# An encoder layer on one core: 35 softmax normalisations on GpSimd, one more pair of projections by half products, and another order of the work

## The chip, the core and the metric

The kernel runs on one core of a Trainium2 chip. Its engines are TensorE (PE, matrix products), VectorE (DVE), ScalarE (ACT) and GpSimd (POOL); SyncE (SP) only issues DMAs, as GpSimd also does. The engines run on their own and wait for each other by semaphores. The time is device microseconds of one execution, and for a kernel the median over its runs.

## What is computed

One layer with two attention mixers side by side, a gated merge, and a SwiGLU block, on 512 tokens of 1024 channels in float32. Cut to what matters here:

```python
proj = h @ w_in[l]                                   # queries, keys, values of both mixers
o_a = windowed_gqa_sink(qa, ka, va, a_sink[l])       # 16 heads, |i-j| <= 128, a learned sink per head
o_b = dilated_mixture(qb, kb, vb)                    # 4 head slots, three dilations each
gates = jax.nn.sigmoid(h @ w_gate[l] + b_gate[l])    # 2 x 1024 channels
mixed = g_a * (o_a @ w_br_a[l]) + g_b * (o_b @ w_br_b[l])
h = layer_norm(DN_ALPHA * h + mixed @ w_out[l], ...)
f = (silu(h @ w_ff_gate[l]) * (h @ w_ff_up[l])) @ w_ff_down[l]
h = layer_norm(DN_ALPHA * h + f, ...)
```

## The kernel before

**Precision.** Every float32 factor is split into a high part that PE takes and a low part (`split`, `parts`: a copy on ScalarE or VectorE, and a subtraction on VectorE, L558, L413, L387). A product of two factors is then three matrix products: high by high, high by low, low by high (L537 to L539, L659 to L661 and so on).

**Units.** The weights come as units of 128 output columns. A unit is computed either alone (`feat_k`, L537 to L539: 8 blocks of the inner dimension x 3 products of 512 columns), or two units at a time by seven half products in place of eight (`pair_x`, L659 to L661: 7 x 12 products of 256 columns). A pair needs sums of weights, which are made by VectorE or by DMAs of GpSimd that add on arrival (L401, L624), and sums of results on VectorE.

**Mixer A.** `unit_a` handles four heads and 128 queries, 16 times. For each head: scores on PE (L903, L904); GpSimd writes the sink's value into a column of the tile (L1065); VectorE adds the mask and takes the row's extreme (L1067); ScalarE takes the exponential and its sum (L1071). When all four heads are there, VectorE takes the reciprocals (L1074), and `normalise` multiplies each head's block by its factor, on ScalarE (L1006) or on VectorE (L1008). Then PE transposes the four blocks together, one piece of 128 keys after the other (`turned_probs`, L1018), ScalarE and VectorE split what comes out (L387, L1023), and PE multiplies by the values (L1084, L1085). GpSimd's queue sends the result to memory (L1091).

**Mixer B.** `unit_b` does one head slot, four times, with eight blocks to normalise; its transposes are L1018 and L1033.

**After the mixers.** `gate` computes a gate unit and its tanh; the second half of the gates is parked in memory until it is used. `branch_a` and `branch_b` multiply the mixers' outputs by their weights and by the gates; then come the output projection (L1549 to L1551), the layer norm, and the SwiGLU block with its own half products (L1759 to L1761, L1970 to L1972).

**What sets the order.** The program is first recorded as operations with the tiles that they read and write. `Program.run` then walks through them with a table of costs and gives each operation a place on an engine: of those whose inputs are ready and whose buffers fit, the one with the lowest priority number. Where an operation lists several engines, the first one free takes it. So the order on each engine is fixed when the program is built, and every engine works through its own in that order. The string `ORDER` names the steps: `P:` and `D:` are pairs by half products (with `D:` their sums are made by DMA), `q`, `k`, `Q`, `K` projections, `g` gates, `R` and `r` rotary turns, `A0` to `A3` four blocks of mixer A, `B0` to `B3` the slots of mixer B, `O` fetches of A's output. The number behind `@` shifts a step's priorities; `BRANCHES` names the order of the branch tiles.

Of the kernel before, what the change touches and what calls it, by code (L numbers as in the profile page):

```python
# [15 lines left out]
P = 128  # L16
# [35 lines left out]
BIAS = 0.2  # L52
SPARE, SPARE2 = (4, 12)
ROOMS = {2: dict(whl=16), 3: dict(whl=20, ws=8)}
# [32 lines left out]
ORDER = """  # L87
X@-11 VA@-23 q2@-799 q1@-877 P:q3,g@-124 R@-106 D:k1,q4@-31 R@155 P:q5,Q01@-843 A0@-168 D:q6,q7@-47 D:g,g@-34 r@631 P:g,Q00@-22 L@-4 A2@-96
D:g,K00@-31 A1@-48 R@187 V12@-20 P:g,K01@-67 R@-5 P:Q02,K02@-28 A3@-55 V0@55 R@5 B0@-7 B1@11 O@25 O@35 P:K10,Q10@-39 O@-13 O@-54 K11@-34 R@24
O@11 P:Q12,Q11@-30 g@28 K12@-12 O@950 g@25 r O@43 P:g,g@-2 B2@-525 O@-304 B3@21 g@-29 P:g,g@-32 g@-8  # L90
"""
FORMS = -255.0
VAL = 140.0
OA_AFTER = (1, 0, 0, 0, 0, 1, 0, 0)
# [9 lines left out]

BRANCHES = "a0 a1 a2 a3 a4 b0 a5 b1 b2 a6 b3 b4 a7 b5 b6 b7"

# [31 lines left out]
class Program:  # L138


    def __init__(self, limits):
        self.limits = limits
        self.used = {k: 0 for k in limits}
        self.ops = []
        self.writer, self.readers = {}, {}
        self.T = 0.0
        self.spare = SPARE
        self.strict = self.hold = False
        self.rooms = {}

# [4 lines left out]
    def op(self, alts, fn, reads=(), writes=(), prio=0.0, after=(), abs_prio=None, moves=0.0, extra=0, table=None):  # L155
# [29 lines left out]
        self.ops.append(o)  # L185
        return o

    def fits(self, o):
# [18 lines left out]
    def run(self):  # L207
# [27 lines left out]
        while n_left:  # L235
# [13 lines left out]
            while progress:  # L249
                progress = False  # L250
                for e in engines:
# [19 lines left out]
                    for b in o.bufs:  # L271
                        if b.tile is None:
                            if b.keys[0] in self.rooms:
                                b.room = self.rooms[b.keys[0]].popleft()
# [70 lines left out]
def hybrid_layer(ctx: ExitStack, tc: tile.TileContext, wpack, xT, xtok, sink, bgate,  # L345
# [24 lines left out]
    def bank(cls):  # L370
        return Buf("bank", cls, lambda r: psum.tile([P, S], F32, tag=f"bank{r}", bufs=1, name=name("ps")))
# [120 lines left out]
    for j in range(2):  # L492
        for w, u in (("k", U_KA), ("q", U_QA), ("v", U_VA), *((i, U_GATE + 8 + i) for i in range(N_ALONG))):
            first[w, j] = half_unit_by(u, j, ((0, S),) if j else ALONG_CUTS if w in range(N_ALONG) else CUTS, FIRST[w, j])
# [52 lines left out]
    def feat_x(ps, wu):  # L547
        for k in range(KD):
            feat_k(ps, wu, k, XM, xtok_of)
# [208 lines left out]

    def in_sbuf(u):

        ps, t = bank("dense"), slot()
        feat_x(ps, unit(u))
        op([(ACT, act(S, True))], lambda e: copy(ACT, halves(t.t), back(ps.t)), reads=[ps], writes=[(t, 1), (t, 2)], prio=EV)
        return t
# [238 lines left out]
    def normalise(p_of, tok, n, f_of, ftok):  # L1003
        def go(e):
            if e == ACT:
                nc.scalar.activation(p_of(), p_of(), AF.Copy, scale=f_of())  # L1006
            else:
                nc.vector.tensor_scalar(p_of(), p_of(), f_of(), None, op0=ALU.mult)  # L1008

        op([(ACT, act(n, extra=1)), (DVE, dve(n, True, 0.06))], go, reads=[tok, ftok], writes=[tok])  # L1010

# [271 lines left out]
    def gate_of(f, t):  # L1283
        gz[f] = t
        op([(ACT, act(S, False, 1))], lambda e: nc.scalar.activation(
            t.t, t.t, AF.Tanh, bias=bg.t[:, f:f + 1], scale=0.5), reads=[(t, 1), (t, 2), bg], writes=[t], prio=EV)
        if f in AWAY:
            put_away(f)
# [6 lines left out]
    def gate(f, ps=None):  # L1295
        if ps is None:
            ps = bank("dense")
            feat_x(ps, unit(U_GATE + f))
        t = slot()
        gz[f] = t  # L1300
        op([(ACT, act(S, True, 1))], lambda e: nc.scalar.activation(
            halves(t.t), back(ps.t), AF.Tanh, bias=bg.t[:, f:f + 1], scale=0.5),
           reads=[ps, bg], writes=[t], prio=EV)
        if f in AWAY:
            put_away(f)
# [6 lines left out]
    def dense_k(u, nt):  # L1312
        ps = bank("dense")
        feat_x(ps, unit(u))
        return k_post(ps, nt) if nt else k_pairs(ps)

    psk, psq, psv = bank("dense"), bank("dense"), bank("dense")
    along = [bank("s") for _ in range(N_ALONG)]
# [11 lines left out]
    for f in range(N_ALONG):  # L1330
        gate(8 + f, ps=along[f])
    ka, qa = {0: k_near(psk, 4)}, {0: q_near(psq, 4, (0, 0))}
    load(mB, maskb, prio=0)
    env = {"gate": N_ALONG, "turn": [], "qs": {}, "ks": {}}

# [29 lines left out]
    def fetch_oa(k):  # L1365
# [8 lines left out]
        return split_of(st, [st], OA_SPLIT, h=Part(xa[k // 4], k % 4) if k >= N_XA else None, by_blocks=True)  # L1374

    def units_of(w):
        i = int(w[1:] or 0)
# [9 lines left out]
        if w[0] == "k":  # L1387
            return U_KA + i, lambda t: ka.update({i: k_post(t, 4)})
        f = (env["gate"] + 8) % 16
        env["gate"] += 1  # L1390
        return U_GATE + f, lambda t: gate_of(f, t)

    def step(w):
        if w == "X":
            x_forms()
        elif w == "L":
            op([(POOL, 0.0)], lambda e: pr.limits.update(ws=N_WS, whl=N_WHL), after=[env["mark"]])
# [31 lines left out]
        elif w[0] in "gG":  # L1429
            for _ in range(int(w[1:] or 1)):  # L1430
                gate((env["gate"] + 8) % 16)
                env["gate"] += 1
        elif w[0] in "QK":
# [16 lines left out]

    for w in ORDER.split():
        w, _, later = w.partition("@")
        pr.T += float(later or 0)
        step(w)
        pr.T -= float(later or 0)
# [5 lines left out]
    op([(POOL, 0.0)], free_all, after=lasts)  # L1461


# [12 lines left out]

    sa.extend(fetch_oa(k) for k in range(len(sa), 8))
    MA = moving(sa)
    sm, sb_ = {}, []

# [13 lines left out]
    def branch_b(f):  # L1494
        if not sb_:
            sb_.extend(split_of(t, [(t, 0), (t, 1)], OB_SPLIT) for t in obT)
        if f % 4 == 0:
            env["wu"] = unit(U_BRB + f // 4)
        MB = moving(sb_)
        ps = bank("dense")  # L1500
        for k in range(2):
            feat_k(ps, env["wu"], k, MB, lambda k: [sb_[k][0].tok, sb_[k][1]], nk=2, col=lambda k: (k, (f % 4) * P))
        mark = gated(8 + f, ps)
# [4 lines left out]

    names = BRANCHES.split()
    marks = []  # L1510
    for n, w in enumerate(names):
        k = 8 + int(w[1])
        if w[0] == "b":
            if k in away:
                fetch_gate(k, [*exps, marks[names.index("b%d" % (k - 11))]] if k > 10 else exps)
        marks.append((branch_a if w[0] == "a" else branch_b)(int(w[1])))
    for w, mark in zip(names, marks):
        env[w] = [mark]


# [594 lines left out]
```

## Time and profile before

| | |
|---|---|
| runs of the kernel before | median 724.24 us of 3 (723.83 to 725.03) |
| the profiled execution | 724.82 us |
| its span, first to last instruction | 723.0 us |
| granted TensorE clock | 0.998 |
| instructions | 14810 |
| HBM read, written | 119.69 MB, 8.39 MB |

The span is what the views divide up. A busy PE in them means that a matrix product is somewhere in its pipeline; the durations of successive products overlap, so the work is read from the distance of their starts. A row of the timeline is: start, duration, engine, line, operation, what it writes and reads, shape. Lines are those of the kernel before.

### The profile page before, as it was taken

What the parts mean: (1) busy time and instruction counts of PE and PEld (TensorE: products, weight loads), DVE (VectorE), ACT (ScalarE), POOL (GpSimd) and SP (SyncE); (2) the same over time, 40 slices, a digit from 0 to 9 for tenths busy, and PEclk for the clock granted to TensorE, in tenths of its full rate; (3) what the DMA queues carried; (4) which work ended last, traced back from release to release, by engine and by line L of the source; (5) the groups of instructions that cost most, each with busy time, mean ns of one, the idle gap of its engine ahead of it and who ended that gap; (6) DMA issues with size and microseconds to landing.
All of it is one profiled execution on the core that took longest, in us unless ns stands there. A gap on an engine that the chain in (4) does not pass through costs nothing.

```text
span 723.0 us, 14810 instructions
## 1 busy us (share of the span) xinstructions
PE 712.5 (99%) x4947; PEld 667.2 (92%) x4947; DVE 664.4 (92%) x1425; ACT 494.6 (68%) x1136; POOL 173.2 (24%) x347
## 2 busy tenths in 40 slices
PE   8999999999999999999999999999999999999996
PEld 6889999998999998988888999999999999999985
DVE  6998999999999989999958998999999999999987
ACT  5768889889878997767625666756567566666821
POOL 0113343322423591550020022121121201212000
PEclk9999999999999999999999999999999999999999
DMA  8978967887568789766690499776897868979402
GB/s 257 294 215 210 235 168 213 227 216 179 137 169 204 187 255 253 219 196 219 199 210 33 110 300 232 177 203 165 238 238 197 223 164 219 253 196 194 106 29 88
DMA packets 81275, 141.44 MB, mean 196 GB/s; under 512 B 11024, under 2 KB 15760, under 8 KB 81200
## 3 DMA queue, kind: packets, MB, share of 16 engines
q1 hardware_dynamic: 63472, 107.07, 46.3%
q0 software_dynamic: 17456, 33.30, 26.6%
q8 instruction: 39, 0.64, 0.4%
q14 instruction: 36, 0.29, 0.1%
q10 hardware_dynamic: 272, 0.13, 0.1%
HBM read 119.69 MB, written 8.39 MB: 177 GB/s over the span
## 4 chain that ended last, share of the span: by engine, by line
PE 90%; DMA 4%; DVE 3%; SPq 2%; ACT 1%; issue 0%; POOL 0%; DVEq 0%; ACTq 0%; POOLq 0%
PE ps L1761 10%; PE ps L1759 10%; PE ps L1760 9%; PE ps L659 5%; PE ps L661 5%; PE ps L660 5%; PE ps L537 4%; PE ps L538 4%; PE ps L539 4%; PE ps L1970 4%; PE ps L1972 4%; PE ps L1971 4%; PE ps L1018 3%; DMA sl<-wpack 3%; PE ps L1549 3%; PE ps L1551 3%
## 5 line engine op out<-in xcount | busy, mean ns | idle before, releaser
L387 ACT ACTIVATE sl<-sl 128x512 fp32r<-128x512 f32 (+3 forms) x457 | 253.8, 588 | 60.7 <-DVE sl L558 43.3
L558 DVE TENSOR_TENSOR sl<-sl,sl 128x512 fp32r<-128x512 f32 (+3 forms) x415 | 245.3, 628 | 6.0 <-ACT sl L387 5.0
L387 ACT ACTIVATE sl<-ps 128x256 f32<-128x256 f32 (+6 forms) x214 | 88.5, 440 | 76.6 <-PE ps L1761 53.0
L401 POOL DMA_DIRECT2D sl<-wpack x70 | 63.0, 931 | 319.1 <-DMA sl<-wpack 92.0
L1760 PE MATMUL ps<-sl,sl 128*128 128x256 f32 x352 | 96.8, 275 | 0.0
L1761 PE MATMUL ps<-sl,sl 128*128 128x256 f32 x352 | 96.8, 275 | 0.0
L1759 PE MATMUL ps<-sl,sl 128*128 128x256 f32 x352 | 96.8, 275 | 0.0
L1759 PE MATMUL ps<-x,sl 128*128 128x256 f32 x264 | 72.6, 275 | 0.0
L1760 PE MATMUL ps<-x,sl 128*128 128x256 f32 x264 | 72.6, 275 | 0.0
L1761 PE MATMUL ps<-x,sl 128*128 128x256 f32 x264 | 72.6, 275 | 0.0
L1759 PEld LDWEIGHTS ps<-sl,sl 128*128 128x128 f32 x352 | 67.6, 192 | 0.1
L1760 PEld LDWEIGHTS ps<-sl,sl 128*128 128x128 f32 x352 | 67.6, 192 | 0.1
L1761 PEld LDWEIGHTS ps<-sl,sl 128*128 128x128 f32 x352 | 67.6, 192 | 0.0
L537 PE MATMUL ps<-x,sl 128*128 128x512 f32 (+1 forms) x161 | 62.1, 386 | 0.7 <-ACT x L387 0.7
L539 PE MATMUL ps<-x,sl 128*128 128x512 f32 (+1 forms) x161 | 60.9, 378 | 0.0
L659 PE MATMUL ps<-sl,sl 128*128 128x256 f32 x208 | 57.8, 278 | 0.9 <-ACT sl L667 0.9
L661 PE MATMUL ps<-sl,sl 128*128 128x256 f32 x208 | 57.3, 276 | 0.0
L660 PE MATMUL ps<-sl,sl 128*128 128x256 f32 x208 | 57.2, 275 | 0.0
L558 DVE TENSOR_TENSOR sl<-sl,ps 128x512 f32<-128x512 f32 (+1 forms) x72 | 47.3, 661 | 9.0 <-PE ps L1972 5.8
L1759 PEld LDWEIGHTS ps<-x,sl 128*128 128x128 f32 x264 | 50.6, 192 | 0.4
L1760 PEld LDWEIGHTS ps<-x,sl 128*128 128x128 f32 x264 | 50.6, 192 | 0.4
L1761 PEld LDWEIGHTS ps<-x,sl 128*128 128x128 f32 x264 | 50.7, 192 | 0.0
(174 smaller groups left out, 2006.6 us busy)
## 6 DMA issues: line engine op xcount, KB each, us to landing
sl<-wpack SPq DMA_DIRECT2D x254, 256.0 KB
sl<-wpack POOLq DMA_DIRECT2D x70, 256.0 KB, 5.5
wf<-wpack SPq DMA_DIRECT2D x51, 256.0 KB
sl<-sl SPq DMA_DIRECT2D x56, 128.0 KB
wf<-wpack POOLq DMA_DIRECT2D x24, 256.0 KB, 5.3
oa<-sl POOLq DMA_DIRECT2D x32, 128.0 KB, 3.6
sl<-sl SPq DMA_DIRECT2D x72, 32.0 KB
gz<-sl SPq DMA_DIRECT2D x8, 256.0 KB
```

What stands on the lines that cost most here:

```text
L387: nc.scalar.activation(dst, src, AF.Copy)
L401: op([(POOL, 1.0)], lambda e: nc.gpsimd.dma_start(b.t, src2, accum_op=ALU.add), reads=[b], writes=[b], prio=prio, moves=1.65)
L537: mm(o, a, x0, start=(k == 0 and begins), stop=False, skip_group_check=split)
L538: mm(o, a, x1, start=False, stop=False, skip_group_check=split)
L539: mm(o, b, x0, start=False, stop=(k == nk - 1), skip_group_check=split)
L558: op([(DVE, dve(w))], lambda e: nc.vector.tensor_tensor(dst(), x(), y(), op=o), reads=reads, writes=writes, prio=prio)
L659: mm(o, wh, pairs(bh[k]()), start=(first and k == 0), stop=False, skip_group_check=True)
L660: mm(o, wh, pairs(bl[k]()), start=False, stop=False, skip_group_check=True)
L661: mm(o, wl, pairs(bh[k]()), start=False, stop=(k == 3), skip_group_check=True)
L1759: mm(o, wh, pairs(bh[k]()), start=(first and k == 0), stop=False, skip_group_check=True)
L1760: mm(o, wh, pairs(bl[k]()), start=False, stop=False, skip_group_check=True)
L1761: mm(o, wl, pairs(bh[k]()), start=False, stop=(k == 3), skip_group_check=True)
```

## The change

`normalise` gets GpSimd as a third engine, with a cost of 0.3 + 0.0012 per column in the planner. `ORDER` is another string: it has 14 pairs by half products in place of 13, it takes the branch tiles (`a0` to `b7`) into itself, and three gates (`g`, and a pair `P:g,g`) stand between branch tiles. The first key and query units (`k0`, `q0`) get steps of their own. `room_for` chooses among free PSUM banks, and all fetched parts of A's output go to plain slots. With the new costs and shifts, the planner puts out another order up to the output projection; the SwiGLU block's order is nearly the same as before. The core of the diff:

```diff
-SPARE, SPARE2 = (4, 12)
+SPARE, SPARE2 = (6, 12)
...
 ORDER = """
-X@-11 VA@-23 q2@-799 q1@-877 P:q3,g@-124 R@-106 D:k1,q4@-31 R@155 P:q5,Q01@-843 A0@-168 D:q6,q7@-47 D:g,g@-34 r@631 P:g,Q00@-22 L@-4 A2@-96
+X@37 P:q3,g@-229 R@-137 VA@-117 D:k1,q4@-42 k0@29 q0@243 R@461 P:q5,Q01@-516 q1@-615 A0@-190 D:q6,q7@-66 r@1309 D:g,g@-75 q2@-543 P:g,Q00@-19
...
+a5@-28 a2@-10 a3@-31 b2 b3@12 b1@-77 a6@-26 a7@-13 b4@23 b7@-75 b5@-71 b6@-207
 """
-FORMS = -255.0
+FORMS = -150.0
...
-STORE, OA, OA_SPLIT, OB_SPLIT, N_OA, N_XA = 0.0, -60.0, -140.0, -140.0, 4, 4
+STORE, OA, OA_SPLIT, OB_SPLIT, N_OA, N_XA = 0.0, -60.0, -140.0, -140.0, 4, 8
...
-BRANCHES = "a0 a1 a2 a3 a4 b0 a5 b1 b2 a6 b3 b4 a7 b5 b6 b7"
...
+    def room_for(self, b):
+        free = self.rooms[b.keys[0]]
+        if b.keys[0] != "bank":
+            return free.popleft()
+        room = next((r for r in free if self.whole.get(r)), free[0]) if b.keys[1] == "d" else free[0]
+        free.remove(room)
+        self.whole[room] = b.keys[1] in ("dense", "o", "d", "dff")
+        return room
...
             if e == ACT:
                 nc.scalar.activation(p_of(), p_of(), AF.Copy, scale=f_of())
+            elif e == POOL:
+                nc.gpsimd.tensor_scalar(p_of(), p_of(), f_of(), None, op0=ALU.mult)
             else:
                 nc.vector.tensor_scalar(p_of(), p_of(), f_of(), None, op0=ALU.mult)
 
-        op([(ACT, act(n, extra=1)), (DVE, dve(n, True, 0.06))], go, reads=[tok, ftok], writes=[tok])
+        op([(ACT, act(n, extra=1)), (DVE, dve(n, True, 0.06)), (POOL, 0.3 + 0.0012 * n)], go, reads=[tok, ftok], writes=[tok])
```

GpSimd's order around the second block of mixer A (`sl_913` is head 0 of the first block, `sl_971` to `sl_977` are the heads of the second), before:

```order
L624 DMA sl_715<-sl_741 128x512
L1065 COPY sl_971<-nsink 128x1
L1065 COPY sl_973<-nsink 128x1
L1065 COPY sl_975<-nsink 128x1
L1065 COPY sl_977<-nsink 128x1
L624 DMA sl_686<-sl_602 128x512
L624 DMA sl_792<-sl_715 128x512
```

The same place after the change; the lines are those of the changed kernel, where L1079 is the copy, L634 the DMA and L1020 the new branch of `normalise`:

```order
L634 DMA sl_716<-sl_742 128x512
L1079 COPY sl_971<-nsink 128x1
L1079 COPY sl_973<-nsink 128x1
L1079 COPY sl_975<-nsink 128x1
L1079 COPY sl_977<-nsink 128x1
L1020 ISA
L1020 TENSOR_SCALAR sl_913<-sl_913,st_926 128x256
L634 DMA sl_682<-sl_602 128x512
L634 DMA sl_792<-sl_716 128x512
L1105 DMA oa_1149<-sl_1129 64x4x128 x2
```

Two rows are new: the first normalisation on GpSimd, and ahead of it an ISA row, which in the built program is a reload of GpSimd's library (index 0). It stands once in the program. The two DMAs behind them are the sums of weights that stood there before.

PE's order at the first transposes of mixer A, before (`ps_1015` is a half product's bank):

```order
L659 MATMUL ps_1015<-sl_419,sl_861 128x256
L660 MATMUL ps_1015<-sl_420,sl_861 128x256
L661 MATMUL ps_1015<-sl_419,sl_862 128x256
L1018 MATMUL ps_1109<-ident,sl_913 128x128
L1018 MATMUL ps_1109<-ident,sl_918 128x128
L1018 MATMUL ps_1109<-ident,sl_922 128x128
L1018 MATMUL ps_1109<-ident,sl_924 128x128
L903 MATMUL ps_1119<-sl_712,sl_596 128x384
L904 MATMUL ps_1119<-sl_713,sl_596 128x384
```

And after, where L669 to L671 are the half products and L1032 the transposes:

```order
L670 MATMUL ps_1037<-x_252,sl_789 128x256
L671 MATMUL ps_1037<-x_244,sl_790 128x256
L1032 MATMUL ps_1062<-ident,sl_913 128x128
L1032 MATMUL ps_1062<-ident,sl_918 128x128
L1032 MATMUL ps_1062<-ident,sl_922 128x128
L1032 MATMUL ps_1062<-ident,sl_924 128x128
L1032 MATMUL ps_1068<-ident,sl_913 128x128
L1032 MATMUL ps_1068<-ident,sl_918 128x128
L1032 MATMUL ps_1068<-ident,sl_922 128x128
L1032 MATMUL ps_1068<-ident,sl_924 128x128
L669 MATMUL ps_979<-sl_330,sl_1001 128x256
```

The transposes of the first block now stand together and earlier: two groups of 12 half products and one head's two score products, which stood ahead of them, stand behind them.

More of the change, by code (lines that the diff above doesn't have):

```diff
@@ L148, in __init__ @@
         self.strict = self.hold = False
-        self.rooms = {}
+        self.rooms, self.whole = {}, {}
     @staticmethod
@@ L492, in hybrid_layer @@
     for j in range(2):
-        for w, u in (("k", U_KA), ("q", U_QA), ("v", U_VA), *((i, U_GATE + 8 + i) for i in range(N_ALONG))):
+        for w, u in (("k", U_KA), ("q", U_QA), ("v", U_VA), *((i, U_GATE + GATES[i]) for i in range(N_ALONG))):
             first[w, j] = half_unit_by(u, j, ((0, S),) if j else ALONG_CUTS if w in range(N_ALONG) else CUTS, FIRST[w, j])
@@ L1286, in gate_of @@
             t.t, t.t, AF.Tanh, bias=bg.t[:, f:f + 1], scale=0.5), reads=[(t, 1), (t, 2), bg], writes=[t], prio=EV)
-        if f in AWAY:
+        if f in AWAY and not env["late"]:
             put_away(f)
@@ L1303, in gate @@
            reads=[ps, bg], writes=[t], prio=EV)
-        if f in AWAY:
+        if f in AWAY and not env["late"]:
             put_away(f)
@@ L1395, in step @@
             x_forms()
+        elif w == "/":
+            late()
+        elif w[0] in "ab":
+            branch(w)
+        elif w in first_of:
+            first_of[w][1](first_of[w][0], False)
+        elif w[1:] in first_of:
+            first_of[w[1:]][1](first_of[w[1:]][0], True)
+        elif w[2:] in first_of:
+            ps, f = first_of[w[2:]]
+            env["turn"].append((in_sbuf(None, ps), lambda t, f=f: f(t, True)))
         elif w == "L":
@@ L1474, in give_room, with branch, late @@
         pr.limits.update(gen=min(pr.limits["gen"] + 1, N_SLOT - N_WS2 - N_WHL))
-    sa.extend(fetch_oa(k) for k in range(len(sa), 8))
-    MA = moving(sa)
-    sm, sb_ = {}, []
+    MA, sm, sb_, marks = [], {}, [], []
+    def branch(w):
+        f = int(w[1:])
+        if w[0] == "b" and 8 + f in away:
+            fetch_gate(8 + f, [*exps, *env["b%d" % (f - 3)]] if f > 2 else exps)
+        marks.append((branch_a if w[0] == "a" else branch_b)(f))
+        env[w] = [marks[-1]]
+    def late():
+        op([(POOL, 0.0)], free_all, after=lasts)
+        sa.extend(fetch_oa(k) for k in range(len(sa), 8))
+        MA.extend(moving(sa))
+        env["late"] = True
     def gated(f, ps):
@@ L1496, in branch_b @@
             sb_.extend(split_of(t, [(t, 0), (t, 1)], OB_SPLIT) for t in obT)
-        if f % 4 == 0:
-            env["wu"] = unit(U_BRB + f // 4)
+        if ("wu", f // 4) not in env:
+            env["wu", f // 4] = unit(U_BRB + f // 4)
         MB = moving(sb_)
@@ L1507, in branch_b @@
         return mark
[L1509 to L1518, printed above, removed]
+    for w in ORDER.split():
+        w, _, later = w.partition("@")
+        pr.T += float(later or 0)
+        step(w)
+        pr.T -= float(later or 0)
     xt = {(t, j): slot() for t in range(NR) for j in range(2)}
```

42 lines of the change are left out of this document (21 added, 21 removed).

## Prediction

> **What bounds the kernel now.** I read the page's first part, the waits of TensorE (PE), the stages by windows, and then the stretch around the first softmax block.
>
> ```profile
> span 723.0 us, 14810 instructions
> PE 712.5 (99%) x4947; PEld 667.2 (92%) x4947; DVE 664.4 (92%) x1425; ACT 494.6 (68%) x1136; POOL 173.2 (24%) x347
> ```
>
> ```profile
> PE ps L473 <- DVE eps L524: 1.2, 1, 1.2
> PE ps L659 <- ACT sl L667: 0.9, 1, 0.9
> PE ps L537 <- ACT x L387: 0.7, 1, 0.7
> PE ps L1018 <- ACT sl L1006: 0.4, 1, 0.4
> ```
>
> ```profile
> 0.00:45.00 45.00, 42.11 (x218) 35.77 (x219) 37.80 (x84) 29.24 (x59) 4.33 (x9) 1.00 0.91 273
> 45.00:240.00 195.00, 195.00 (x1457) 186.22 (x1456) 184.12 (x437) 165.24 (x406) 63.34 (x131) 1.00 0.76 193
> 240.00:280.00 40.00, 39.60 (x288) 37.01 (x287) 36.43 (x97) 34.99 (x92) 25.45 (x70) 1.00 0.89 239
> 280.00:345.00 65.00, 65.00 (x368) 58.51 (x367) 60.12 (x161) 44.87 (x115) 21.10 (x72) 1.00 0.72 214
> 345.00:390.00 45.00, 45.00 (x214) 39.46 (x213) 34.65 (x58) 20.19 (x35) 5.25 (x6) 1.00 0.64 176
> 690.00:723.00 33.00, 25.97 (x121) 22.40 (x119) 25.45 (x46) 4.49 (x9) 0.00 (x0) 0.97 0.17 64
> ```
>
> The columns of the last view are PE, its weight loads (PEld), VectorE (DVE), ScalarE (ACT), GpSimd (POOL), the granted clock and the DMA share. PE is idle for 723.0 - 712.5 = 10.5 us: 2.9 in the first 45, 7.0 in the last 33, almost nothing between, and the clock is full. So the kernel is as long as PE's work. It can gain by less PE work, or by the waits of 3.2 us in all; of these 1.2 is the start. It can lose by any new wait of PE, in full. ScalarE is the engine with room (165 of 195 us); VectorE is full to 184 of 195.
>
> **The change, part by part.** *PE's work.* Over the whole program the order has 48 matrix products of 512 columns less and 84 of 256 columns more: one more pair of units goes by seven half products. Durations of PE overlap, so the price is the distance of starts:
>
> ```profile
> 61.34 0.28 PE L660 MATMUL ps<-sl,sl 128*128 128x256 f32 x1
> 62.46 0.28 PE L661 MATMUL ps<-sl,sl 128*128 128x256 f32 x1
> 62.57 0.38 PE L537 MATMUL ps<-x,sl 128*128 128x512 f32 x1
> 63.22 0.38 PE L537 MATMUL ps<-x,sl 128*128 128x512 f32 x1
> ```
>
> Between the first two rows lie 10 steps, so 0.112 us each; between the last two lie 3, so 0.217. That makes 84 x 0.112 - 48 x 0.217 = 9.4 - 10.4 = -1.0 us.
>
> *ScalarE and VectorE.* ScalarE loses 15 normalisations and VectorE 20; GpSimd gets 35.
>
> ```profile
> L1006 ACT ACTIVATE sl<-sl,st 128x256 f32<-128x256 f32 x32 | 14.6, 497 | 2.2 <-DVE st L1074 2.2
> L1008 DVE TENSOR_SCALAR sl<-sl,st 128x256 f32<-128x256 f32 x24 | 7.7, 348 | 0.1
> L1008 DVE TENSOR_SCALAR sl<-sl,st 128x384 f32<-128x384 f32 x13 | 5.4, 431 | 0.1
> L558 DVE TENSOR_TENSOR sl<-sl,sl 128x512 fp32r<-128x512 f32 x261 | 173.8, 684 | 5.4 <-ACT sl L387 5.0
> ```
>
> VectorE: 14 x 0.348 + 6 x 0.431 = 7.5 us less; the extra pair puts about six operations of 0.684 on it, 4.1 us, and some copies come over from ScalarE. That is near zero in all; ScalarE is freed of about 15 x 0.5 = 7.5 us, which it did not need. Neither shortens PE's work.
>
> *GpSimd's normalisation* is nowhere in the trace. Its bounds are VectorE's 0.348 us below and, above, what GpSimd does now:
>
> ```profile
> L1065 POOL COPY sl<-nsink x64: 173/259/1302, 61.8 to 220.0; 128x1 f32<-128x1 f32 x64
> L1106 POOL MEMSET sl<- x4: 151/174/490, 233.4 to 293.6; 128x64 f32 x4
> L2103 POOL MEMSET const-float32-0.0<- 128x1 f32 x1 | 0.1, 98 | 0.2 <-issue 0.2
> 62.18 0.74 POOL L1065 COPY sl<-nsink 128x1 f32<-128x1 f32 x1
> 62.19 0.69 DVE L558 TENSOR_TENSOR sl<-sl,sl 128x512 fp32r<-128x512 f32 x1
> ```
>
> A copy of one column takes 0.173 us at least (minimum, median, maximum stand in this order), and up to 1.3. The single copy in the fourth row takes 0.74, and it ends 0.04 after the VectorE operation that ran beside it. From a memset of one column (0.098) to the median of 64 columns (0.174) are 0.076 us for 63 columns, 1.2 ns each; so I put 256 columns at 0.173 + 0.31 = 0.48 us and 384 at 0.63, plus up to 0.7 for an operation of VectorE in front: 0.35 to 1.3. The blocks of a unit are shared out over three engines, and ScalarE alone needs 1.30 us for its three (below), so GpSimd's share lies beside it and I let it cost nothing on PE's path.
>
> The Trainium skill's page "SBUF — State Buffer" (section "SBUF: two separate sides") says that GpSimd and VectorE lock a pair of ports against each other for a whole instruction, when VectorE reads two SBUF operands and GpSimd reads SBUF. By that rule the trace agrees (the copy of 0.74 us), and each of the 35 would also hold VectorE up; that is the second rival below.
>
> *The load ahead of the first of them.* GpSimd's order has a new row, ISA, ahead of its first TENSOR_SCALAR, and none later: there the built program reloads GpSimd's library. GpSimd takes it in order, behind the four copies for the second block. In the trace of before, that place looks so:
>
> ```profile
> 68.80 1.26 POOL L1065 COPY sl<-nsink 128x1 f32<-128x1 f32 x4
> 69.80 1.08 POOL L624 DMA_DIRECT2D sl<-sl  x1
> 69.26 0.17 DVE L1074 RECIPROCAL st<-st 128x4 f32<-128x4 f32 x1
> 69.98 0.33 DVE L1008 TENSOR_SCALAR sl<-sl,st 128x256 f32<-128x256 f32 x1
> 70.56 1.30 ACT L1006 ACTIVATE sl<-sl,st 128x256 f32<-128x256 f32 x3
> 76.76 0.60 PE L1018 MATMUL ps<-ident,sl 128*128 128x128 f32 x4
> ```
>
> The factors are there at 69.43 and all four blocks are normalised at 71.86; the first transposes, which need all four, start at 76.76, 4.9 us later. The change puts them earlier on PE: 24 half products (2.7 us) and two score products (0.3 together, since 512 columns take 0.217) that stood ahead now stand behind. So PE reaches them at 73.8. GpSimd's copies end at 70.06; after a load of R and a normalisation of 0.48 the transposes can start at 70.06 + R + 0.48 + 0.1 for the hand-over, and PE, whose next work is all behind them, waits R - 3.2 us. ScalarE and VectorE next evacuate those same transposes, so they wait too, and nothing is made up.
>
> The trace has no load of this kind. The nearest rows are ScalarE's own table load, and GpSimd's transfers from memory at that time:
>
> ```profile
> L387 ACT ACT_TABLE_LOAD x1 | 1.3, 1283 | 1.4 <-PEq L2103 1.4
> L624 POOL DMA_DIRECT2D sl<-sl x8: 854/1108/1242, 60.6 to 133.3; - x8
> DMA to landing us min/median/max: 5.0/5.0/7.5
> 75.00:80.00 5.00, 5.00 (x47) 4.98 (x46) 4.48 (x13) 4.50 (x12) 0.87 (x1) 1.00 0.97 267
> ```
>
> At 1.28 us PE would not wait; a gain from a load is excluded, since it gives PE nothing that it lacked before. As one transfer (0.85 to 1.24 to issue, 5.0 to 7.5 to land) R is 5.9 to 8.7 and PE waits 2.7 to 5.5. As two transfers one behind the other R is about 11.1 and the wait 7.9. I take the single transfer near its slow end, R = 8.2, because the DMA engines are 0.97 busy at that time: a wait of 5.0 us. The Trainium skill's page "GPSIMD Engine Reference" (section 2.1, "Instruction dispatch") puts the first call after a library load at about 6 us, with no row of its own in a profile; as an estimate from that page the wait is 2.8 us and the time 727.0. No run here shows it yet.
>
> Behind the load on GpSimd's queue stand two weight sums (the DMA of the second row above), the stores of the first block and the next copies. The first sum is needed on PE about 11 us of products after the first transposes, at 89.8 if they start at 78.8. Issued at about 78.8 it lands after 1.1 + 7.5, at 87.4, and is split by two operations of 0.6 to 0.7: 88.8. It fits by 1 us, so I price it at nothing, or a few us if the landing slips.
>
> *The rest.* Three gates are computed between the branch tiles, where PE was busy 45.00 of 45 (345 to 390): nothing to gain there, and nothing lost while their tanh on ScalarE (20 of 45 busy) has room. The other moved products keep the same counts. The two waits of 0.9 and 0.4 may go or come back elsewhere; GpSimd's share of later blocks may come late. I put +1.0 on all this, between -1.3 (both waits gone) and +4.
>
> *Sum.* 723.0 - 1.0 + 5.0 + 1.0 = 728.0 us of span. The profiled execution took 724.82 with that span, 1.8 more, which makes 729.8; it is 0.6 above the median of the three runs (724.24), so the forecast is 729.
>
> **The rivals.** *The load is hidden, and the kernel gets faster.* If R is under 3.2 us, as a table load's 1.28 is, PE waits for nothing, keeps the 1.0, and at best drops the two waits too: 724.2 - 1.0 = 723.2, down to 721.9. It decides at R = 4.2, where the wait equals the gain. For it speaks that only GpSimd's queue has to carry the load, which is 24% busy; against it that anything fetched through the DMA engines there took 5.0 us and more.
>
> *VectorE becomes the bound.* 24 x 0.48 + 11 x 0.63 = 18.5 us of normalisations read SBUF. If VectorE stands still through all of them, its 280.7 busy us (184.12 + 36.43 + 60.12) of the 300 between 45 and 345 become 299, and PE waits for it.
>
> ```profile
> 36.00:54.00 18.00, 17.09 (x126) 16.12 (x125) 17.75 (x34) 11.22 (x22) 2.71 (x4) 1.00 0.77 215
> 342.00:360.00 18.00, 18.00 (x85) 15.77 (x84) 18.00 (x31) 10.25 (x17) 0.00 (x0) 1.00 0.58 189
> ```
>
> A VectorE as full as that cost PE 0.91 us of 18 once and nothing another time: 0 to 15 us over 300. I take a quarter, 4: 733 with the load, 727 without it. The lock is seen in the copies; against it, a copy never held VectorE up visibly, and only a part of VectorE's operations read two SBUF operands. That the normalisations are not moved at all is excluded: 35 stand in GpSimd's order.
>
> **How the numbers follow.** The load seen by PE as priced: 0.60. VectorE the bound: 0.14. The load hidden or nearly so: 0.26, of which 0.18 end more than 0.2% (1.4 us, about what a measurement of this kernel can tell) below the time before and 0.08 within it. So faster 0.18, same 0.08, slower 0.74. The range begins at 722.5, inside the hidden case, with about 0.1 below it; its top is two transfers (729 + 2.9) and a full VectorE (+4), 736.
>
> **What would show it.** In the profile after, PE should have one new wait of about 5 us at its first transposes (L1032), ended by POOL's L1020, with GpSimd free of rows for R us in front of it; and the half products x84, the 512-column products less by 48. Right but mis-sized: the same wait of another length. Wrong: no wait there; or many small waits of PE on transposes, with VectorE at 97% and more between 45 and 345; or a POOL TENSOR_SCALAR of over 1.3 us as a rule.

## The result, and the profile after

The changed kernel took 740.51 us (median of 4, 739.30 to 743.58), the kernel before 724.63 on the same chip (median of 4, 723.83 to 725.04): a ratio of 1.0227, interval 1.0214 to 1.0240. That is 15.9 us slower, outside the range of 722.5 to 736 that was forecast. The direction was forecast; the cause was another.

The page's first part for the kernel after, and its waits of TensorE (engine, tile and line <- whom it waited for: us in total, times, the longest):

```profile
span 738.7 us, 14971 instructions
PE 716.4 (97%) x4983; PEld 668.6 (91%) x4983; DVE 671.8 (91%) x1423; ACT 490.6 (66%) x1115; POOL 225.9 (31%) x384
```

```profile
PE ps L1032 <- POOL sl L1020: 8.9, 9, 2.0
PE ps L1047 <- POOL sl L1020: 2.6, 3, 1.2
PE ps L669 <- ACT sl L677: 0.9, 1, 0.9
```

In place of one long wait at the first transposes there are twelve, 11.5 us in all, spread from 106 to 350 us, all of transposes (L1032, L1047) on GpSimd's normalisation (L1020). The profiled execution took 740.63 us with this span, 15.8 more than that of before (724.82).

The place where the library load was expected, GpSimd's rows and the first transposes on TensorE (start, duration, engine, line):

```profile
68.74 1.23 POOL L1079 COPY sl<-nsink 128x1 f32<-128x1 f32 x4
69.82 1.14 POOL L1020 TENSOR_SCALAR sl<-sl,st 128x256 f32<-128x256 f32 x1
73.85 1.04 PE L1032 MATMUL ps<-ident,sl 128*128 128x128 f32 x8
```

Between the copies and the first normalisation there is no gap. What the order shows as ISA is two rows in the trace:

```profile
L1020 POOLq MODIFY_POOL_CONFIG  x2: 233/233/233, 69.7 to 69.7; - x2
```

They take 0.23 us each on GpSimd's sequencer, side by side. The normalisation ends at 70.96, and TensorE comes to the transposes at 73.85, where the prediction had put it (73.8). Here the load costs nothing. In other kernels of this series the two rows took up to 1.50 us and the first normalisation behind them up to 3.28 (both in the kernel of before with 35 on GpSimd); no wait of TensorE on it stands there either.

The price was elsewhere. GpSimd's groups by form (instructions, busy us, mean ns of one), and then all 35 with minimum, median and maximum:

```profile
L1020 POOL TENSOR_SCALAR sl<-sl,st 128x256 f32<-128x256 f32 x21 | 30.2, 1442 | 13.4 <-DVE st L1088 10.7 <-DVE st L1194 2.3 <-DMA sl<-wpack 0.2
L1020 POOL TENSOR_SCALAR sl<-sl,st 128x384 f32<-128x384 f32 x11 | 19.6, 1783 | 18.3 <-DVE st L1088 18.3
L1020 POOL TENSOR_SCALAR sl<-sl,st 128x192 f32<-128x192 f32 x3 | 2.8, 934 | 6.3 <-DVE st L1194 6.3
L1020 POOL TENSOR_SCALAR sl<-sl,st x35: 763/1383/2943, 69.8 to 349.4; 128x256 f32<-128x256 f32 x21, 128x384 f32<-128x384 f32 x11, 128x192 f32<-128x192 f32 x3
```

The planner reckons with 0.3 us + 1.2 ns a column: 0.76 us for a block of 384, and 0.61 for the others, since it takes the three of 192 for 256 columns too; that is 22.9 us for the 35. They took 52.6. The worst place on the chain of waits, in order of time (start, us, what):

```profile
132.87 4.94 issue
137.87 6.70 POOL sl L1020 x3
144.57 0.04 issue
144.62 0.88 PE ps L1032 x6
```

Three blocks that one reciprocal of VectorE releases (a row of one factor, in what follows) stand one behind the other on GpSimd. They start when their factor is there and take 6.70 us, where the planner reckons 3 x 0.76 = 2.3; the transposes that TensorE has next start 0.05 us after the last of them. Ten such rows of two to four blocks, one behind the other without a gap, hold 25 of the 35 normalisations, and eleven of the twelve waits end with the second or a later block of a row.

The stages by windows (PE, weight loads, VectorE, ScalarE, GpSimd, clock, DMA share) show that VectorE is not the bound: in the long stage it is busy 176.1 of 195 us, where it was 184.1 before, and TensorE has lost 6.1.

```profile
45.00:240.00 195.00, 188.92 (x1400) 178.63 (x1399) 176.10 (x400) 153.83 (x373) 92.88 (x144) 1.00 0.74 185
280.00:345.00 65.00, 62.94 (x367) 55.88 (x366) 57.92 (x159) 47.54 (x116) 32.35 (x98) 1.00 0.84 228
```

### The profile page after: what moved, and what is told of

Its sections match the earlier page's. It is cut to its first block, busy times and chain, and to the rows that moved or that the text cites. A ratio compares the mean times of both kernels' runs of the same rounds, so it can differ in the third digit from the quotient of the medians.

```text
span 738.7 us, 14971 instructions
## 1 busy us (share of the span) xinstructions
PE 716.4 (97%) x4983; PEld 668.6 (91%) x4983; DVE 671.8 (91%) x1423; ACT 490.6 (66%) x1115; POOL 225.9 (31%) x384
## 4 chain that ended last, share of the span: by engine, by line
PE 76%; POOL 7%; DMA 6%; DVE 3%; issue 3%; ACT 2%; SPq 2%; DVEq 0%; POOLq 0%; ACTq 0%
PE ps L1784 9%; PE ps L1785 9%; PE ps L1786 9%; DMA sl<-wpack 4%; POOL sl L1020 4%; PE ps L1995 4%; PE ps L1997 4%; PE ps L1996 4%; PE ps L669 4%; PE ps L670 4%; PE ps L671 3%; PE ps L1575 3%; PE ps L1576 3%; PE ps L1574 3%; PE ps L547 3%
## 5 line engine op out<-in xcount | busy, mean ns | idle before, releaser
L397 ACT ACTIVATE sl<-sl 128x512 fp32r<-128x512 f32 (+3 forms) x464 | 258.1, 589 | 51.8 <-DVE sl L568 24.5
L568 DVE TENSOR_TENSOR sl<-sl,sl 128x512 fp32r<-128x512 f32 (+3 forms) x424 | 252.5, 630 | 4.0 <-ACT sl L397 3.1
L397 ACT ACTIVATE sl<-ps 128x256 f32<-128x256 f32 (+3 forms) x200 | 85.2, 444 | 85.7 <-PE ps L1786 52.7
L1785 PE MATMUL ps<-sl,sl 128*128 128x256 f32 x352 | 96.8, 275 | 0.0
L1786 PE MATMUL ps<-sl,sl 128*128 128x256 f32 x352 | 96.8, 275 | 0.0
L1784 PE MATMUL ps<-sl,sl 128*128 128x256 f32 x352 | 96.8, 275 | 0.0
L1020 POOL TENSOR_SCALAR sl<-sl,st 128x256 f32<-128x256 f32 (+2 forms) x35 | 52.5, 1505 | 37.9 <-DVE st L1088 29.0
L669 PE MATMUL ps<-sl,sl 128*128 128x256 f32 x224 | 62.2, 277 | 0.9 <-ACT sl L677 0.9
L671 PE MATMUL ps<-sl,sl 128*128 128x256 f32 x224 | 61.7, 275 | 0.0
L670 PE MATMUL ps<-sl,sl 128*128 128x256 f32 x224 | 61.6, 275 | 0.0
L423 DVE TENSOR_TENSOR sl<-sl,sl 128x512 fp32r<-128x512 f32 x70 | 46.6, 683 | 1.8 <-ACT sl L397 1.4
```

Source lines behind the costliest of these rows:

```text
L397: nc.scalar.activation(dst, src, AF.Copy)
L423: op([(DVE, dve(S))], lambda e: nc.vector.tensor_tensor(l.t, src.t, f32(h.t), op=ALU.subtract), reads=[src, h], writes=[l], prio=prio, abs ...
L568: op([(DVE, dve(w))], lambda e: nc.vector.tensor_tensor(dst(), x(), y(), op=o), reads=reads, writes=writes, prio=prio)
L669: mm(o, wh, pairs(bh[k]()), start=(first and k == 0), stop=False, skip_group_check=True)
L670: mm(o, wh, pairs(bl[k]()), start=False, stop=False, skip_group_check=True)
L671: mm(o, wl, pairs(bh[k]()), start=False, stop=(k == 3), skip_group_check=True)
```

## The experiments

Theory L: TensorE loses because the GpSimd normalisations themselves end late, and transposes stand behind them. Theory V: GpSimd's use of the port that it shares with VectorE, and its queue, hold the others up. Theory O: the new order of the program is itself worse. "Before" means the kernel before, run on the same chip; its medians were 724.4 to 724.7.

**The 35 on ScalarE.**

```
-            if e == ACT:
+            if e in (ACT, POOL):
                 nc.scalar.activation(p_of(), p_of(), AF.Copy, scale=f_of())
```

> Order of after kept to the instruction; the 35 normalisations that it gives to GpSimd are issued on ScalarE at the same places (there one of 256 columns takes 0.50 us, on GpSimd it took 1.44). Theory L, GpSimd's normalisations end too late for TensorE's transposes and nothing else of the change costs: 721 to 727 us, and the waits of the transposes on the normalisation (11.5 us in all in after) fall under 3. Theory O, the new order is itself worse: 735 or more. Theory V, GpSimd's port work and its queue hold VectorE and the copies up: recovers like L, 721 to 728, so this run does not part L from V.

Measured 730.42 us, ratio 1.0081 (1.0066 to 1.0096). That lies between the forecasts, and all three ranges miss it: 10 of the 16 us go, 6 stay.

```profile
PE ps L1045 <- ACT sl L1018: 1.3, 3, 0.5
PE ps L1030 <- ACT sl L1018: 0.9, 2, 0.6
```

The transposes (two lines further up in this kernel) wait 2.2 us for ScalarE, where they waited 11.5 for GpSimd; that part of L holds. What the other 3.6 us over before are, this run does not say.

**Half the columns.**

```
-  nc.gpsimd.tensor_scalar(p_of(), p_of(), f_of(), None, op0=ALU.mult)
+  nc.gpsimd.tensor_scalar(p_of()[:, :n // 2], p_of()[:, :n // 2], f_of(), None, op0=ALU.mult)
```

> After with GpSimd normalising only the first half of each block's columns, so half of those probabilities stay unnormalised. The shortest GpSimd normalisations of after fit 0.30 us and 2.4 ns a column; by that line half the columns take 0.53, 0.61 and 0.76 us when alone, the very prices in the planner. L: most of the lateness goes, what is left is waiting ahead of the port: 725 to 731 us. O: 737 or more. V, if it is the number of port turns that counts and not their length: 735 or more.

Measured 738.78 us (735.69 to 741.13), ratio 1.0206 (1.0181 to 1.0231): hardly better than after, and L's 725 to 731 missed. (Of the three blocks of 192 columns the kernel multiplies 128.)

```profile
L1020 POOL TENSOR_SCALAR sl<-sl,st 128x128 f32<-128x128 f32 x24 | 27.2, 1139 | 23.9 <-DVE st L1088 13.9 <-DVE st L1194 9.8
L1020 POOL TENSOR_SCALAR sl<-sl,st 128x192 f32<-128x192 f32 x11 | 14.9, 1356 | 16.9 <-DVE st L1088 16.9
PE ps L1032 <- POOL sl L1020: 6.1, 7, 1.4
PE ps L1047 <- POOL sl L1020: 1.2, 1, 1.2
```

Half the columns took not half the time but four fifths (42.1 us in all for 52.6). So L as I had put it, with the length of the columns as the main thing, was wrong: most of an instruction's surplus does not go with its columns. The waits fell to 7.3 us in the profiled execution, which was the shortest of the four (735.69 us). Its granted clock was 0.997, as in after; in the other three it was 0.992. At the clock of after, in this one execution, the gain is 4 to 5 us, as the waits say, and not the 1.7 of the medians; why the clock was lower in the others, no trace shows.

**Before with 35 on GpSimd.**

```
+            turn[0] += 35
+            if turn[0] >= 96:
+                turn[0] -= 96
+                nc.gpsimd.tensor_scalar(p_of(), p_of(), f_of(), None, op0=ALU.mult)
-            if e == ACT:
+            elif e == ACT:
```

> Order of before kept; 35 of its 96 normalisations, evenly spread over the call, are issued on GpSimd at the places where ScalarE or VectorE had them. L: the normalisation's end moves out by some 0.9 us each with a median slack of about 0.9 us at the transposes, as in after or worse, for no plan allows for it: 733 to 752 us. O, the new order is what costs: 723 to 727. V: 730 to 745.

Measured 733.47 us, ratio 1.0122 (1.0107 to 1.0137): with none of the new order, GpSimd's normalisations cost 8.8 us, at the lower end of L's range. O's 723 to 727 falls as an account of the whole loss; V's 730 to 745 holds as well as L's.

```profile
PE ps L1023 <- POOL sl L1009: 4.1, 4, 2.9
PE ps L1038 <- POOL sl L1009: 2.6, 2, 1.5
```

Spread evenly, they stand less often two or three in a row. But four of these six waits, 5.7 of 6.7 us, end with a normalisation that stands alone. The longest is in mixer B, where the normalisation has other work of GpSimd's own ahead of it, some ten us of small copies, of which this is the last:

```profile
267.20 0.70 POOL L1169 COPY st<-st 32x2 f32<-32x2 f32 x1
268.00 0.92 POOL L1009 TENSOR_SCALAR sl<-sl,st 128x256 f32<-128x256 f32 x1
268.98 0.99 PE L1023 MATMUL ps<-ident,sl 128*128 128x128 f32 x7 [2.87 <-POOL sl L1009]
```

**A shadow on GpSimd, first try.** The kernel of the first experiment, with a multiplication on a scratch tile at the same places; the clearing of that tile was given to the planner as one more operation.

> The first of these kernels (normalisations on ScalarE in after's order) and, at the same 35 places, a GpSimd multiplication of the same size on a scratch tile that nobody reads: it holds the port and GpSimd's queue as in after, and no transposes wait for it. L: within 2 us of the kernel without it. V, the holding of the port and of the queue costs by itself: 6 us or more above it.

Measured 758.03 us, ratio 1.0454 (1.0438 to 1.0471). It does not decide: the added operation made the planner find another order (28 places instead of 35, and TensorE's waits stand elsewhere). The next kernel does it without touching the plan.

**Nobody waits for GpSimd.**

```
-  nc.gpsimd.tensor_scalar(p_of(), p_of(), f_of(), None, op0=ALU.mult)
+  if not started:
+      started.append(nc.gpsimd.memset(scratch, 0.0))
+  nc.gpsimd.tensor_scalar(scratch[:, :n], scratch[:, :n], f_of(), None, op0=ALU.mult)
```

> Order of after kept. At its 35 places GpSimd multiplies a scratch tile of the block's size instead of the block (one clearing of that tile ahead of the first): port, queue and the wait for the factor as in after, but the transposes no longer wait for GpSimd; those 35 blocks stay unnormalised. Theory L (TensorE loses by waiting for the late normalisation itself): 722 to 729 us, within 3 us of the kernel that leaves the 35 out. Theory V (holding the port and the queue slows the others): 733 to 740, as after.

Measured 728.12 us, ratio 1.0050 (1.0035 to 1.0065). GpSimd's instructions are as long as in after:

```profile
L1023 POOL TENSOR_SCALAR scratch<-scratch,st 128x256 f32<-128x256 f32 x24 | 34.5, 1437 | 19.2 <-DVE st L1197 7.8 <-DVE sl L399 5.2 <-DVE st L1091 5.0
L1023 POOL TENSOR_SCALAR scratch<-scratch,st 128x384 f32<-128x384 f32 x11 | 19.1, 1741 | 16.2 <-DVE st L1091 15.8
```

They hold the port and the queue just as long, and 12.4 us are gone. V falls as a cost of its own; that the transposes wait for them is the loss. (VectorE's share in how long they are is another question, taken up with the prices below.)

**The 35 left out.** The same branch holds `pass`.

> Order of after kept, the 35 GpSimd normalisations left out altogether (those blocks stay unnormalised): what the new order takes when they cost nothing. L: 721 to 726 us, and the 5.8 us that stayed with ScalarE in their place came of ScalarE being late there. O, the new order itself is worse: 728 to 732, hardly under the 730.4 of ScalarE in their place.

Measured 727.41 us, ratio 1.0045 (1.0031 to 1.0058), within a microsecond of the kernel above. It is 2.9 us over before, a little under O's 728 and above L's 726: the new order costs that much even with these normalisations for nothing.

**The rest alone, planned afresh; and the planner told the true price.** In the first the planner has no GpSimd for a normalisation; in the second:

```
-  (POOL, 0.3 + 0.0012 * n)
+  (POOL, 0.8 + 0.0024 * n)
```

> The change without its GpSimd part: the planner has only ScalarE and VectorE for the normalisations and plans afresh; half products, gates between branch tiles and all else as in after. L: 720 to 726 us, TensorE's work being 1 us less than before. O, those other parts cost by themselves: 728 to 734.

> After with the planner's price of a GpSimd normalisation set from the trace: 0.8 us and 2.4 ns a column (1.41 us for 256 columns, measured mean 1.44; it was 0.3 us and 1.2 ns, 0.61). The planner then gives GpSimd 14 blocks or so in place of 35 and places them for their true length. L: 721 to 728 us, the transposes' waits on GpSimd under 3 us in all. V, each costs by the port: 40% of the loss stays, 728 to 732.

Measured 737.96 us, ratio 1.0178 (1.0156 to 1.0199), and 742.44, ratio 1.0246 (1.0230 to 1.0262). All ranges missed, those of L, O and V. With the true price the planner gave GpSimd 27 blocks (not 14, as I had thought), and the transposes' waits on them are down to 0.5 us, but TensorE waits elsewhere:

```profile
PE ps L1154 <- DVE st L1138: 3.5, 1, 3.5
PE ps L1047 <- POOL sl L1020: 0.5, 1, 0.5
```

Either the other parts of the change are bad, or every new plan is. The next kernel asks this of the kernel before, in which none of the change stands.

**Before with one price moved.**

```
-  (DVE, dve(n, True, 0.06))
+  (DVE, dve(n, True, 0.16))
```

> The kernel before, nothing of the change in it, with one price of its planner moved: a normalisation on VectorE 0.10 us dearer. The plan comes out otherwise, the numbers of the order's table stay. Theory T, the table's numbers fit only the prices that they were found with, and that is why the change planned afresh without GpSimd took 738 and with true prices 742: some 4 to 15 us slower than before, 728 to 740. Rival, the other parts of the change cost those 13 us: this kernel stays at 723 to 727.

Measured 742.41 us, ratio 1.0250 (1.0233 to 1.0267), a little worse than T's range. Not all of the 18 us is TensorE waiting: for 13.7 us the granted clock is 0.50, which takes up to 6.9 us (that stretch, in the columns of the windows above):

```profile
302.90:316.60 13.70, 10.22 (x32) 8.37 (x33) 10.41 (x30) 8.05 (x19) 5.25 (x31) 0.50 0.82 227
```

In the profiles of before and after it is 1.00 up to 700 us. In this one trial the order's table fits only the prices that it was found with, and a plan made afresh cannot be used to price one part of this change. The experiments that keep an order are the ones that count.

**Only the first of each row on GpSimd.** `last` remembers the factor of the normalisation before.

```
+            first = e == POOL and last[0] is not ftok[0]
+            if e == POOL:
+                last[0] = ftok[0]
-            if e == ACT:
+            if e == ACT or e == POOL and not first:
```

> Order of after kept. Of the normalisations that one factor releases, which stand in a row on GpSimd, the first stays there (19 of the 35); the other 16 are issued on ScalarE. Theory R, the lateness is that of the rows, two to four normalisations one after the other behind one factor: nearly all of it goes that ScalarE's own lateness does not bring back, 729 to 733 us. Rival E, each GpSimd normalisation costs alike: of the 12.4 us between after and the kernel that nobody waits in, 19/35 stay, and ScalarE's share comes on top: 735 to 738.

Measured 731.07 us, ratio 1.0089 (1.0072 to 1.0107). R holds, E falls: with 19 of the 35 still on GpSimd the transposes' waits on it are 0.5 us, once.

```profile
PE ps L1035 <- POOL sl L1023: 0.5, 1, 0.5
```

**No normalisation at all, in both orders.** All three branches hold `pass`.

> The kernel before, its order kept, all 96 normalisations left out (the probabilities stay unnormalised): what the cheapest normalisation could bring. Theory B, TensorE's work bounds the kernel and its waits on the normalisations were 0.4 us: 722.5 to 724.5, so nothing was to be had from it. Rival, VectorE's and ScalarE's time at the normalisations does hold the kernel up: under 721.

> Order of after kept, all 96 normalisations left out. If the 2.9 us that the new order costs with GpSimd's 35 left out stands in the remaining 61 being late on ScalarE and VectorE, this falls to the 722 to 723 that TensorE's 1 us less would give; if it stands in the rest of the order, it stays at 726 to 728.

Measured 723.97 us, ratio 0.9994 (0.9985 to 1.0003), as theory B had it, and 727.39, ratio 1.0034 (1.0023 to 1.0046). Nothing was to be had from cheaper normalisations in the kernel before. And the 2.9 us of the new order do not stand at the normalisations, for they stay without any. In its trace one wait is new, of products on a VectorE operation behind the transposes:

```profile
PE ps L1218 <- DVE sl L1052: 2.1, 2, 1.6
```

**The prices by themselves.** Three kernels compute nothing of the layer. In the first, VectorE's rows mostly did not stand beside the blocks that they were meant for:

> No part of the layer is computed: GpSimd multiplies a block of 128, 192, 256, 384 and 512 columns, eight times each, with VectorE idle, and then eight blocks of 256 columns beside a row of 24 VectorE instructions of one kind: difference of two SBUF tiles, difference of PSUM and SBUF, copy out of PSUM, copy from SBUF to SBUF, multiplication of 256 columns (512 columns but for the last). Theory P, GpSimd waits while VectorE holds the port that they share: alone 0.30 us and 2.4 ns a column (0.61, 0.76, 0.91, 1.22, 1.53), beside some kinds of VectorE work 1.3 us or more and beside others 0.91. Rival: GpSimd's own time wanders, 1.2 us or more for 256 columns also when alone.

It gave 1.25 us for 384 columns and 1.58 for 512 with VectorE idle: the price of P, and the same each time, so that the rival falls. The blocks of 128, 192 and 256 columns ran beside the row of SBUF differences, which all write one tile and so wait for each other (0.03 us between one and the next). There they took 0.79, 0.85 and 0.92 us, and for 256 columns that is the time alone (0.93 below):

```profile
L378 DVE TENSOR_TENSOR vc<-va,vb 128x512 f32<-128x512 f32 x6 | 5.2, 863 | 0.2
L368 POOL TENSOR_SCALAR gb<-gb,one 128x256 f32<-128x256 f32 x3 | 2.8, 919 | 0.0
```

The difference is the one that grew, from 0.69 us to 0.86, and one of each went by every 0.90 us. The second fixed the order and left VectorE no gaps:

> No part of the layer is computed. As the first kernel of prices, but with the order fixed by hand, so that each kind of VectorE work does run beside GpSimd's eight blocks of 256 columns, and with the 24 VectorE instructions writing four tiles in turn, so that they follow each other without a gap. Theory P, in the layer GpSimd waits for the end of a row of VectorE instructions that read two SBUF tiles, and not for those that read PSUM: a GpSimd multiplication takes up to 10 us or more beside a row of SBUF differences, up to 4 us or more beside the copies from SBUF to SBUF, 0.92 beside PSUM differences and PSUM copies. Rival, they take turns one by one: at most 1.3 us each beside any of them.

Its groups in four of its windows, 256 columns each time: alone, beside differences of two SBUF tiles, beside differences of PSUM and SBUF, beside copies from SBUF to SBUF.

```profile
L369 POOL TENSOR_SCALAR ga<-ga,one 128x256 f32<-128x256 f32 x4 | 3.7, 928 | 0.7 <-DVE one L379 0.7
...
L382 DVE TENSOR_TENSOR vc<-va,vb 128x512 f32<-128x512 f32 x17 | 11.9, 774 | 0.0
L369 POOL TENSOR_SCALAR ga<-ga,one 128x256 f32<-128x256 f32 x4 | 5.7, 1435 | 1.1 <-DVE one L379 1.1
...
L383 DVE TENSOR_TENSOR vc<-pa,vb 128x512 f32<-128x512 f32 x13 | 7.9, 679 | 0.0
L369 POOL TENSOR_SCALAR ga<-ga,one 128x256 f32<-128x256 f32 x4 | 3.7, 928 | 4.4 <-DVE one L379 4.4
...
L385 DVE COPY vc<-va 128x512 f32<-128x512 f32 x24 | 11.0, 535 | 0.0
L369 POOL TENSOR_SCALAR ga<-ga,one 128x256 f32<-128x256 f32 x4 | 5.6, 1396 | 7.4 <-DVE one L379 7.4
```

The kinds are as P has them: 0.93 us alone and beside PSUM, 1.43 and 1.40 beside differences and copies that read SBUF alone. One kind was left out of P: beside VectorE's own multiplications by a factor, 256 columns from SBUF to SBUF, GpSimd takes 0.95, and VectorE is the one held up, with 0.53 us where one takes 0.35 by itself. The waiting for whole rows is not as P has it: two SBUF differences go by for each multiplication, which is 0.5 us longer. That comes to the layer's mean for 256 columns (1.44 us), though the layer's VectorE work is a mixture of all these kinds and no run sorted it. The third varied the columns, beside SBUF differences:

> No part of the layer is computed; as the kernel of prices beside, with rows of 28 VectorE instructions: GpSimd blocks of 128, 192, 384 and 512 columns beside SBUF differences of 512 columns, 384 beside SBUF copies, 256 beside SBUF differences of 256 columns, and 256 beside differences and copies mixed. Theory once, GpSimd waits once for its turn: each length takes its time alone (0.61, 0.77, 1.25, 1.57) and 0.50 us more, so 1.75 for 384. Theory share, it is held up again as it goes: the surplus grows with the columns, 0.75 or more for 384, 1.0 for 512. Neither gives the 1.2 to 1.7 us of the worst in the layer, unless the mixed row does.

```profile
L369 POOL TENSOR_SCALAR ga<-ga,one 128x128 f32<-128x128 f32 x4 | 5.4, 1354 | 0.9 <-DVE one L379 0.9
...
L369 POOL TENSOR_SCALAR ga<-ga,one 128x384 f32<-128x384 f32 x4 | 8.5, 2129 | 6.8 <-DVE one L379 6.8
...
L369 POOL TENSOR_SCALAR ga<-ga,one 128x512 f32<-128x512 f32 x4 | 9.2, 2288 | 2.0 <-DVE one L379 2.0
```

Neither forecast holds: the surplus over the time alone is about 0.7 us at 128 columns, 0.5 at 256, 0.88 at 384 and 0.7 at 512. It does not go with the columns. That it comes in steps of VectorE's instructions fits two more rows, 256 columns beside differences half as long (1.22 us, a surplus of 0.3) and 384 beside copies (1.65, 0.4), but no run shows it by itself. This also explains the kernel with half the columns: beside VectorE, 128 columns take 1.35 us and 256 take 1.43, so halving saves next to nothing there. The row of differences and copies mixed gave 1.16 to 1.54, so the longest in the changed kernel (2.94 us for 384 columns, 2.53 for 256) are not reproduced; why they took 0.8 to 1.1 longer still stays open.

## Why the prediction was wrong

*What bounds the kernel: right.* "The kernel is as long as PE's work" and "can lose by any new wait of PE, in full": without any normalisation the kernel before takes 723.97 us, so nothing was to be gained there, and the 11.5 us of new waits came out as 12.4 in the time.

*GpSimd's normalisation: the step that failed*, with "I let it cost nothing on PE's path". Two things in it were wrong. Its price: 0.48 and 0.63 us stood against 1.44 and 1.78 measured. The slope came from a memset (1.2 ns a column), and a multiplication alone takes 0.93 at 256 columns and 1.25 at 384, 2.5 ns a column; beside VectorE's SBUF differences without gaps it takes 0.5 to 0.9 more. The upper bound of 1.3 was below the median of 1.38. And its cover: one block for GpSimd beside three for ScalarE was taken as the rule, but the planner, believing in 0.61 us, put two to four of one factor in a row on GpSimd. With the rows broken up, the waits on GpSimd fall from 11.5 us to 0.5, and the kernel (731.07, with 16 of the blocks on ScalarE) is within noise as long as the one with none on GpSimd (730.42). How much of this the slower price alone would have cost is not shown. Nor is a single block free everywhere: in the order of before, four single ones made 5.7 us of waits.

*The load: wrong.* The forecast's 5.0 us did not come. The rows for the bound were transfers through the DMA engines; what stands there takes 0.23 us. The Trainium skill's page "GPSIMD Engine Reference" (section 2.1, "Instruction dispatch") expects about 6 us at the first call of a freshly loaded kernel; the trace differs, 0.23 us and a first call of 1.14, and decides. Whether any code had to be fetched for this library, no run shows. That the forecast had the right sign is owed to this step in part, and so to a wrong reason.

*PE's work and the rest.* The -1.0 us lies in the number of products and their distances, and no run measured it by itself; the order that brings it, with its normalisations free, is 2.9 us slower than before. So "the rest" was 2.9 + 1.0 = 3.9 us where +1.0 was put, just inside its bound of +4. The new waits that I found in it are 2.1 us, two of one kind. Without any normalisation TensorE is idle for 2.2 us between 45 and 390, where it was 0.4 in the kernel before, and from the start of its last product to the end are 8.3 us instead of 7.5; the remainder was not followed.

*The sum with measured terms:* -1.0 for PE's work, 0 for the load, 12.4 for the waits on GpSimd, 3.9 for the rest, 15.3 us; measured 15.9. This is a division of the loss and no test of it: the 12.4 is after less the kernel in which nobody waits, and -1.0 with 3.9 is the kernel with the 35 left out less before, so the sum had to come near. What bears it out is the 11.5 us of waits that the trace of after names.

*The rivals.* "VectorE becomes the bound" falls: VectorE is busy for 272 of the 300 us between 45 and 345, where it was 281, and holding the port without anybody waiting costs 0.7 us, which is not clear of noise (728.12 against 727.41, intervals that overlap). The many small waits that it had as its sign came without it. "The load is hidden" was true, but the gain that hung on it did not come. The profile that would make the prediction wrong was named: "a POOL TENSOR_SCALAR of over 1.3 us as a rule" is what came.

## What to carry to other kernels

When TensorE has no idle time, moving work that nobody waits for to a slower engine has nothing to win and can lose: first leave that work out altogether and see what it could bring (here 0.5 us, within the measurement). Price an operation that the trace lacks by running it alone and beside its neighbours, and add up what stands in a row behind one releaser, and what else stands ahead of it on that engine, since the bottleneck waits for the later ones. Where a plan is tuned to its prices, compare variants within one fixed order, or the plan's own scatter (here 18 us for one price moved by 0.1, up to 6.9 of them at half clock) hides what is asked.

## What the runs showed of the hardware

GpSimd's multiplication by a factor per partition, alone, in the second kernel of prices:

```profile
L369 POOL TENSOR_SCALAR ga<-ga,one 128x512 f32<-128x512 f32 x4 | 6.3, 1568 | 0.7 <-DVE one L379 0.7
...
L369 POOL TENSOR_SCALAR ga<-ga,one 128x384 f32<-128x384 f32 x4 | 5.0, 1248 | 0.7 <-DVE one L379 0.7
...
L369 POOL TENSOR_SCALAR ga<-ga,one 128x128 f32<-128x128 f32 x4 | 2.4, 609 | 0.9 <-DVE one L379 0.9
```

From 128 to 512 columns are 0.96 us, 2.5 ns a column. Beside differences of two SBUF tiles without gaps 128, 256, 384 and 512 columns take 1.35, 1.43, 2.13 and 2.29 us (rows above); beside differences that wait for each other 256 columns take 0.92, and VectorE is slowed instead. The Trainium skill's page "SBUF — State Buffer" (section "SBUF: two separate sides") has the two engines exclude each other for a whole instruction. The kinds of VectorE work that delayed GpSimd in the second kernel of prices agree with it, and PSUM work did not delay it (0.93). The length does not agree: a row of seven SBUF differences with GpSimd idle has one every (4.29 - 0.68) / 6 = 0.60 us,

```profile
64.56 4.29 DVE L382 TENSOR_TENSOR vc<-va,vb 128x512 f32<-128x512 f32 x7
```

and eight multiplications of 0.93 with 16 such differences took 11.3 us (53.24 to 64.54), not 8 x 0.93 + 16 x 0.60 = 17.0. The first kernel of prices says the same: a multiplication of 0.92 us and a difference of 0.86 went by every 0.90. For a part of its instruction GpSimd runs beside VectorE.
